# Moving the modulation's vector work between the stages of a two-layer transformer kernel

## The chip, the cores and the metric

The kernel runs on one core of a Trainium2 chip. The number that counts is the device time of one execution in microseconds. The work of one core is shared by five engines that run at the same time and wait for one another by semaphores: PE (TensorE, matrix products), DVE (VectorE, elementwise), ACT (ScalarE, elementwise and functions), POOL (GpSimd) and SP (SyncE, which here only issues the loads). [...]

## The reference, cut to what matters

The reference computes two layers over two streams of 256 tokens, the latent `lat` and the context `cx`, with 1024 channels. Every layer begins with modulation vectors, nine pieces of 1024 for each stream, which come from one large product; they give shift, scale and gate of the layer's three blocks.

```
for i in range(2):
    mod  = (silu(c)     @ mod_w[i] + mod_b[i]).reshape(bsz, 3, 3, 1, 1024)     # mod_w[i]: 1024 x 9216
    modc = (silu(c_ctx) @ mod_w[i] + mod_b[i]).reshape(3, 3, 1024)
    lat = lat + 0.5 * mod[:, 0, 2] * swiglu(modulate(lat, norm_g[i, 0], mod[:, 0, 0], mod[:, 0, 1]), w13[i, 0], w2[i, 0])
    ...                                               # the same for cx
    y   = short_conv_mixer(...)  if i == 0 else  gqa_mixer(...)
    lat = lat + mod[:, 1, 2] * y
    lat = lat + 0.5 * mod[:, 2, 2] * swiglu(modulate(lat, ...), w13[i, 1], w2[i, 1])

modulate(t, g, shift, scale) = rms(t, g) * (1 + scale) + shift
swiglu(h, w13, w2)           = (silu(gate) * up) @ w2,   gate, up = split(h @ w13)      # hidden 2816
```

Layer 0 has the convolution, layer 1 the attention (8 query heads of 128, 2 key heads, keys from both streams). The context is dropped after the attention of layer 1, so the last swiglu works on 256 tokens and every other on 512. All of it is in float32.

## The kernel before, in words

**Products.** Channels lie on the 128 partitions and tokens along the free axis. To keep float32 accuracy on PE, every operand is split into a high and a low half (`split`, L97 to L99: a copy on ACT makes the high half, a subtraction on DVE the low half), and one product is three matmuls (`mm3`, L122 to L124: high by high, high by low of the activations, low of the weights by high). A weight tile is loaded raw (`load_raw`, tiles `wr`, 1 MB each, three buffers, issued by SP), and its halves `wh` and `wl` (L98, L99) are the tiles that PE reads.

**Stages.** In order of time: a startup in which the first modulation pieces are computed on PE and the first norm is applied in four quarters (`norm_q`, which calls `norm_k`, L264 to L275), with PE's order written out by hand in `FIRST_STEPS`; swiglu (0, 0); the convolution, eight blocks of channels in one loop; its output projection; swiglu (0, 1); swiglu (1, 0); the attention with its projections; the projection by `wo`; and the last swiglu (1, 1).

**A swiglu** (`ffn`) has 22 blocks of 128 hidden channels, taken in thirds of 8, 7 and 7 (`THIRDS`). Each third makes its blocks of silu(gate) * up and then projects them back by `w2` (`project`). A block is made in one of two ways. Plain: 48 matmuls of 512 columns. As a block pair (class `Pair`): seven products of 256 columns, twelve matmuls each, in place of the eight half-products of a plain block; the operands are sums of weight blocks and sums of activation blocks. A pair's weight sums are made on DVE (`ws`, L564, L570, L574), then split like the others, so that PE does less for a pair and DVE more. The first third of swiglu (0, 0) has eight plain blocks: three that end the startup, and five of the loop `AS_IS`. The first third of (0, 1) and of (1, 0) has two plain blocks and six pairs, every later third has seven pairs. The last swiglu has plain blocks of 256 columns alone. So there are 14 pairs in (0, 0) and 20 each in (0, 1) and (1, 0), 54 in all.

**The modulation.** All pieces but the first two are computed on DVE, beside the rest. One operation (`mod_unit`, the tile `junk`, L142) multiplies a 128 x 1024 piece of the weights by silu(c) and adds along the row. There are 224 of them. A load of 1 MB (`modT`, through the same three `wr` buffers and the same SP queue as the other weights) feeds four of them, or two where only the latent stream needs the piece. Where they stand in the program is set by `tick(n)`: it adds n to what is owed, and issues as many whole operations as are owed. `mod_ready` issues whatever is missing before a piece is read. Ticks stand in the plain blocks' loop (L660), after the startup (L852), after each of the eight blocks of the convolution (L903), in `project` (argument `ev`, once for each of its first six or eight tiles), and in the attention (L1133, after each head, and a few others).

The order in the program is not the order on the engine. A scheduler places every engine's instructions by estimated readiness, and takes the program's order as priority; only PE's order in the startup is fixed by hand.

**The attention's heads** (L1127 to L1133). A head's scores go PE (`psc`), DVE (`mx`, `nb`), ACT (`e`, the exponential), DVE (`r`), POOL (`pn`, L1088, the only large use of POOL), PE (`pt`, a transpose), ACT and DVE (`pth`, `ptl`, the split), PE (`pav`). There are 16 such half heads. The weights of the projection that follows are split on DVE and ACT in the same time.

Of the kernel before, what the change touches and what calls it, by code (L numbers as in the profile page):

```python
# [20 lines left out]
T2 = 2 * S  # L21
# [20 lines left out]
def hybrid_kernel(ctx: ExitStack, tc: tile.TileContext, a: dict, out: bass.AP):  # L42
# [126 lines left out]
    def next_unit():  # L169
        if not units:  # L170
            l, ch, pair = jobs.pop(0)
            mod_tile(l, ch)
            raw = load_raw(a["modT"][l, ch * 4 + pair])
            units.extend(
                (l, ch, pair, raw, j, v) for j in range(2) for v in range(streams(l, ch))
            )
        mod_unit(*units.pop(0))

    def tick(n):

        owed[0] += n
        while (jobs or units) and owed[0] >= 1:
            owed[0] -= 1
            next_unit()
# [109 lines left out]
    def pick(h, k, c0, c1):  # L294
        return h.at(k, c0, c1)
# [92 lines left out]
    def new_pair(s):  # L388

        return (  # L390
            gp.tile([P, T2], F32R, name=nm(s + "h"), tag="gh"),
            gp.tile([P, T2], F32R, name=nm(s + "l"), tag="gl"),
        )
# [224 lines left out]
    def ffn(l, b, h, tot, gate, tail, gs=(), ev=1.5):  # L618
        gs = list(gs)
        i0 = 0  # L620
        for t, n in enumerate(THIRDS):
            between = ()
            if tot == T2:
                heads = []
                if t == 0 and not gs:

                    w = [load_w(a["w13"][l, b, 0])]
                    gs = [new_pair("g") for _ in range(2)]
                    pp = [(psum("pg"), psum("pu")) for _ in range(2)]
                    w13_mm(pp[0], w[0], h, range(KT), 0, S)  # L630
                    flush()
                    w.append(load_w(a["w13"][l, b, 1]))
                    w13_mm(pp[1], w[1], h, range(KT), 0, S)
                    h.sums(0)
                    w13_mm(pp[0], w[0], h, range(KT), S, T2)
                    w13_post(pp[0], gs[0], 0, T2)
                    heads.append(Pair(a["w13"][l, b, 2], h))
                    h.sums(1)
                    heads[0].sums(0)
                    w13_mm(pp[1], w[1], h, range(KT), S, T2)  # L640
                    w13_post(pp[1], gs[1], 0, T2)
                    heads[0].head()
                    h.sums(2)
                    heads[0].sums(1)
                prev = None
                for i in range(len(gs), n):
                    if t == 0 and not heads and i in AS_IS[l, b]:
                        w = load_w(a["w13"][l, b, i])
                        pp = psum("pg"), psum("pu")
                        if prev:  # L650
                            prev.seven()
                        w13_mm(pp, w, h, range(4), 0, T2)
                        if prev:
                            gs.append(new_pair("g"))
                            prev.four(gs[-1])
                            prev = None
                        w13_mm(pp, w, h, range(4, KT), 0, T2)
                        gs.append(new_pair("g"))
                        w13_post(pp, gs[-1], 0, T2)
                        tick(5)  # L660
                        continue
                    if heads:
                        pr = heads.pop(0)
                    else:
                        pr = Pair(a["w13"][l, b, i0 + i], h)
                        pr.sums(0)
                        pr.sums(1)
                        pr.head()
                    pr.five()
                    if prev:  # L670
                        prev.seven()
                    pr.six()
                    if prev:
                        gs.append(new_pair("g"))
                        prev.four(gs[-1])
                    prev = pr

                def last():
                    gs.append(new_pair("g"))
                    prev.four(gs[-1])  # L680

                between = (prev.seven, last) if prev else ()
            else:
                for i in range(n):
                    w = load_w(a["w13"][l, b, i0 + i])
                    gs.append(new_pair("g"))
                    pp = psum("pg"), psum("pu")
                    w13_mm(pp, w, h, range(KT), 0, tot)
                    w13_post(pp, gs[i], 0, tot)
                    tick(1)  # L690
            i0 += n
            box = {}

            def ws2(m):
                if m // 2 not in box:
                    src = a["w2a"][l, b, m // 2] if t == 0 else a["w2b"][l, b, t - 1, m // 2]
                    box[m // 2] = load_raw(src, 2 * n * P)
                raw = box[m // 2]
                o = (m % 2) * n * P
                hi, lo = half()  # L700
                split(hi[:, : n * P], lo[:, : n * P], raw[:, o : o + n * P])
                return lambda k: (hi[:, k * P : k * P + P], lo[:, k * P : k * P + P])

            cur = gs
            end = t == len(THIRDS) - 1
            project(
                ws2, lambda k, c0, c1: (cur[k][0][:, c0:c1], cur[k][1][:, c0:c1]), n,
                gate, tail if end else None, tot, 2 if end and tot == T2 else 0, ev, between,
            )
            gs = []  # L710

    def lazy_gate(l, j):
        box = []

        def get():
            if not box:
                box.append(gate_of(l, j))
            return box[0]

        return get  # L720


    h = Plain()
# [123 lines left out]
    h = FirstBlocks(h, h32)  # L847
# [1 line left out]
        gs0.append(new_pair("g"))  # L849
        w13_post(pps[i], gs0[i], 0, T2)  # L850
    h.sums()
    tick(6)  # L852

    convk = cload("convk", [P, 3, KT])
    qg = cload("qg", [P, 1])
# [5 lines left out]
    hn = Plain()  # L861
    ffn(0, 0, h, T2, lazy_gate(0, 0), tail_norm(0, 1, hn), gs0, 1.8)
    h = hn

    zs = []
    for m in range(KT):
        wcx = load_w(a["cw_cx"][m])
        if m % 2 == 0:
            wb = load_w(a["cw_b"][m // 2])
        pc, pv, pb = psum("pc"), psum("pv"), psum("pb")  # L870
        for c0, c1 in ((0, S), (S, T2)) if m == 0 else ((0, T2),):
            groups = ((pv, wcx, P), (pc, wcx, 0), (pb, wb, (m % 2) * P))
            if m == 0:
                order = [(k, *g) for k in range(KT) for g in groups]
            else:
                order = [(k, *g) for g in groups for k in range(KT)]
            for n, (k, ps, w, off) in enumerate(order):
                mm3(ps[:, c0:c1], w(k * 256 + off), pick(h, k, c0, c1), k == 0, k == KT - 1)
                if n == 11:
                    flush()  # L880
        xv = tp.tile([P, T2], F32, name=nm("xv"), tag="sg", bufs=3)
        nc.scalar.copy(xv, pv)
        u = tp.tile([P, T2], F32, name=nm("u"), tag="gm", bufs=3)
        nc.vector.tensor_tensor(out=u, in0=xv, in1=pc, op=ALU.mult)
        d = tp.tile([P, T2], F32, name=nm("d"), tag="gm", bufs=3)
        nc.vector.tensor_scalar(
            out=d, in0=u, scalar1=convk[:, 1, m : m + 1], scalar2=None, op0=ALU.mult
        )
        u2 = u.rearrange("p (s t) -> p s t", s=2)
        d2 = d.rearrange("p (s t) -> p s t", s=2)  # L890
        nc.vector.scalar_tensor_tensor(
            out=d2[:, :, 1:], in0=u2[:, :, : S - 1], scalar=convk[:, 0, m : m + 1],
            in1=d2[:, :, 1:], op0=ALU.mult, op1=ALU.add,
        )
        nc.vector.scalar_tensor_tensor(
            out=d2[:, :, : S - 1], in0=u2[:, :, 1:], scalar=convk[:, 2, m : m + 1],
            in1=d2[:, :, : S - 1], op0=ALU.mult, op1=ALU.add,
        )
        z = tp.tile([P, T2], F32, name=nm("z"), tag="sg", bufs=3)
        nc.vector.tensor_tensor(out=z, in0=d, in1=pb, op=ALU.mult)  # L900
        zs.append(new_pair("z"))
        split(zs[m][0], zs[m][1], z)
        tick(6)  # L903

    def by_pairs(key):
        box = {}
# [9 lines left out]
    hn = Blocks()  # L916
# [4 lines left out]
    h = hn  # L921
    hn = Blocks()
    ffn(0, 1, h, T2, lazy_gate(0, 2), tail_norm(1, 0, hn), (), 1.7)
    h = hn


    hn = Plain()
    ffn(1, 0, h, T2, lazy_gate(1, 0), tail_norm(1, 1, hn), (), 1.6)
    h = hn
    ap = ctx.enter_context(tc.tile_pool(name="ap", bufs=2))  # L930

# [195 lines left out]
    for hd in range(HEADS):  # L1127
        if hd + 2 < HEADS:
            pns[hd + 2] = scores(hd + 2)
        pts[hd] = turn(pns.pop(hd))  # L1130
        if hd:
            mix(hd - 1, pts.pop(hd - 1))
        tick(0.75)  # L1133
    mix(HEADS - 1, pts.pop(HEADS - 1))


    hn = Plain(S)
# [87 lines left out]
```

## Time and profile before

| what | value |
|---|---|
| time, median of 3 runs | 1597.02 us (1593.21 to 1598.21) |
| the profiled execution | 1595.53 us, its span 1593.7 us |
| PE busy | 1568.8 us, 98% of the span |
| DVE busy | 1303.3 us, 82% |
| ACT busy | 721.1 us, 45% |
| POOL busy | 29.4 us, 2% |
| modulation operations | 224, mean 1281 ns, 286.9 us of DVE |

A span is the time between the first and the last instruction of the profiled execution; the time of the run is 1.8 us longer. Busy shares are taken over the whole span. They say which engine has the most work, not where it stands still, and a stage can be bound by another engine than the whole: a stage's own busy times are read from a view by windows of time. In the views, "idle before" names what ended the idle time in front of a group of instructions.

### The profile page before, as it was taken

How to read it: one execution, taken by the hardware profiler on the slowest of the kernel's cores; microseconds unless marked ns; L12 is line 12 of the kernel's file. 1: busy time of each engine (PE TensorE's matmuls, PEld its weight loads, DVE VectorE, ACT ScalarE, POOL GpSimd, SP SyncE). 2: the span in 40 equal slices, each digit the busy share in tenths (PEclk: the TensorE clock that was granted, in tenths of full speed). 3: DMA queues.
4: the chain of work that ended last, by engine and by line, in shares of the span. 5: the costliest groups of instructions: out<-in, count | busy, mean ns of one | idle time of the engine just before them, and what ended most of it. 6: DMA issues, size and time to landing. Idle time of an engine off the chain costs nothing.

```text
span 1593.7 us, 25820 instructions
## 1 busy us (share of the span) xinstructions
PE 1568.8 (98%) x10666; PEld 1449.7 (91%) x10666; DVE 1303.3 (82%) x1984; ACT 721.1 (45%) x1103; POOL 29.4 (2%) x20
## 2 busy tenths in 40 slices
PE   8999999999999999999999999999999998899999
PEld 7688998999888899989899899899899897899999
DVE  5998888979999879798798879898797789876554
ACT  6522452544322356335345365335255455644443
POOL 0000000000000000000000000000000005200000
PEclk9999999999999999999999999999999999999999
DMA  9465324334565522452342513443433554556452
GB/s 359 181 238 207 110 99 153 133 102 176 177 219 195 175 68 93 148 170 100 129 156 96 180 56 107 158 136 99 169 118 120 208 186 151 200 185 220 166 200 102
DMA packets 39575, 248.79 MB, mean 156 GB/s; under 512 B 5409, under 2 KB 7201, under 8 KB 14625
## 3 DMA queue, kind: packets, MB, share of 16 engines
q1 hardware_dynamic: 36864, 245.38, 43.9%
q10 hardware_dynamic: 2592, 1.76, 0.4%
q8 instruction: 83, 1.36, 0.3%
q14 instruction: 36, 0.29, 0.1%
HBM read 244.77 MB, written 1.05 MB: 154 GB/s over the span
## 4 chain that ended last, share of the span: by engine, by line
PE 92%; DVE 4%; ACT 2%; DMA 1%; issue 0%; POOL 0%; ACTq 0%; DVEq 0%; POOLq 0%
PE py L123 10%; PE py L122 10%; PE py L124 10%; PE p L124 7%; PE p L123 7%; PE p L122 6%; PE q L122 5%; PE q L124 5%; PE q L123 5%; PE pg L122 2%; PE pg L124 2%; PE pg L123 2%; PE pu L124 2%; PE pu L123 2%; PE pu L122 2%; PE pv L122 1%
## 5 line engine op out<-in xcount | busy, mean ns | idle before, releaser
L98 ACT ACTIVATE wh<-wr 128x1024 fp32r<-128x1024 f32 (+2 forms) x276 | 276.4, 1014 | 388.0 <-PE py L123 140.7
L99 DVE TENSOR_TENSOR wl<-wr,wh 128x1024 fp32r<-128x1024 f32 (+2 forms) x276 | 319.9, 1166 | 88.2 <-ACT wh L98 87.9
L142 DVE CUSTOM_DVE_ANT_0 junk<-wr,scbc,modb 128x1024 bf16<-128x1024 f32 x224 | 286.9, 1281 | 31.8 <-DMA wr<-in_modT 29.0
L122 PE MATMUL py<-gh,wh 128*128 128x512 f32 (+1 forms) x746 | 263.3, 353 | 0.0
L123 PE MATMUL py<-gl,wh 128*128 128x512 f32 (+1 forms) x746 | 263.0, 353 | 0.0
L124 PE MATMUL py<-gh,wl 128*128 128x512 f32 (+1 forms) x746 | 262.7, 352 | 0.0
L99 DVE TENSOR_TENSOR wl<-ws,wh 128x1024 fp32r<-128x1024 f32 x108 | 131.6, 1223 | 34.1 <-ACT wh L98 34.0
L124 PEld LDWEIGHTS py<-gh,wl 128*128 128x128 f32 x746 | 141.1, 189 | 19.0
L122 PEld LDWEIGHTS py<-gh,wh 128*128 128x128 f32 x746 | 141.2, 189 | 18.6
L123 PEld LDWEIGHTS py<-gl,wh 128*128 128x128 f32 x746 | 141.2, 189 | 18.1
L98 ACT ACTIVATE wh<-ws 128x1024 fp32r<-128x1024 f32 x108 | 113.9, 1058 | 71.3 <-PE p L123 44.5
L124 PE MATMUL p<-th,wl 128*128 128x256 f32 x432 | 122.3, 283 | 0.0
L123 PE MATMUL p<-tl,wh 128*128 128x256 f32 x432 | 122.2, 283 | 0.0
L122 PE MATMUL p<-th,wh 128*128 128x256 f32 x432 | 122.2, 283 | 0.0
L453 DVE SCALAR_TENSOR_TENSOR x<-py,G,x 128x256 f32<-128x256 f32 x168 | 73.9, 477 | 23.1 <-PE py L124 23.1
L122 PE MATMUL q<-bh,wh 128*128 128x256 f32 x320 | 90.6, 283 | 0.0
L123 PE MATMUL q<-bl,wh 128*128 128x256 f32 x320 | 90.6, 283 | 0.0
L124 PE MATMUL q<-bh,wl 128*128 128x256 f32 x320 | 90.6, 283 | 0.0
L122 PEld LDWEIGHTS p<-th,wh 128*128 128x128 f32 x432 | 82.9, 192 | 0.3
L123 PEld LDWEIGHTS p<-tl,wh 128*128 128x128 f32 x432 | 82.9, 192 | 0.3
L124 PEld LDWEIGHTS p<-th,wl 128*128 128x128 f32 x432 | 82.9, 192 | 0.0
L124 PE MATMUL pg<-hh,wl 128*128 128x256 f32 (+1 forms) x240 | 75.5, 315 | 2.8 <-DVE wl L99 2.7
(236 smaller groups left out, 4045.2 us busy)
## 6 DMA issues: line engine op xcount, KB each, us to landing
wr<-in_w SPq DMA_DIRECT2D x88, 1024.0 KB, 4.9
wr<-in_modT SPq DMA_DIRECT2D x64, 1024.0 KB, 5.0
wr<-in_w2b SPq DMA_DIRECT2D x32, 896.0 KB, 4.6
wr<-in_w2a SPq DMA_DIRECT2D x16, 1024.0 KB, 4.9
pm<-in_mod SPq DMA_DIRECT2D x16, 512.0 KB, 10.0
wr<-in_cw_cx SPq DMA_DIRECT2D x8, 1024.0 KB, 4.9
wr<-in_cw_b SPq DMA_DIRECT2D x4, 1024.0 KB, 5.0
wr<-in_cw_out SPq DMA_DIRECT2D x4, 1024.0 KB, 4.9
```

What stands on the lines that cost most here:

```text
L98: nc.scalar.activation(out=hi, in_=src, func=AF.Copy)
L99: nc.vector.tensor_tensor(out=lo, in0=src, in1=hi.bitcast(F32), op=ALU.subtract)
L122: nc.tensor.matmul(ps, wh, mh, start=first, stop=False, **kw)
L123: nc.tensor.matmul(ps, wh, ml, start=False, stop=False, **kw)
L124: nc.tensor.matmul(ps, wl, mh, start=False, stop=last, **kw)
L142: nc.vector.tensor_tensor_reduce(out=junk, in0=raw[:, j * D : j * D + D], in1=scbc[:, v, :], scale=1.0, scalar=modb[:, l, col : col + 1], ...
L453: nc.vector.scalar_tensor_tensor(out=x[:, m, s * S : s * S + S], in0=ps[:, o : o + S], scalar=g[:, m, s : s + 1], in1=x[:, m, s * S : s * ...
```

## The change

Five places differ. In the plain blocks of the swiglus four operations of the modulation are issued after a block where there were five; this loop runs five times, in swiglu (0, 0). After each of the 54 block pairs a new half operation is owed, so one is issued after every second pair, 27 in all. After the startup four are issued where there were six; after each block of the convolution five where there were six; in the projections of swiglu (1, 0) 1.4 for each tile where there were 1.6 (22 tiles). After each attention head 0.75 was owed, six in all, and now none. Counted in the program's order these are 5 + 2 + 8 + 4.4 + 6 = 25.4 operations taken away and 27 added; the number of operations, of loads and of all other instructions on every engine is the same, since the last pieces are simply reached earlier or later.

```diff
@@ -657,7 +657,7 @@   (ffn, the plain blocks)
                         gs.append(new_pair("g"))
                         w13_post(pp, gs[-1], 0, T2)
-                        tick(5)
+                        tick(4)
                         continue
@@ -674,6 +674,7 @@   (ffn, the block pairs)
                         gs.append(new_pair("g"))
                         prev.four(gs[-1])
                     prev = pr
+                    tick(0.5)
@@ -849,7 +850,7 @@   (after the startup)
     h.sums()
-    tick(6)
+    tick(4)
@@ -900,7 +901,7 @@   (the convolution's loop)
         split(zs[m][0], zs[m][1], z)
-        tick(6)
+        tick(5)
@@ -925,7 +926,7 @@
-    ffn(1, 0, h, T2, lazy_gate(1, 0), tail_norm(1, 1, hn), (), 1.6)
+    ffn(1, 0, h, T2, lazy_gate(1, 0), tail_norm(1, 1, hn), (), 1.4)
@@ -1130,7 +1131,6 @@   (the attention's heads)
             mix(hd - 1, pts.pop(hd - 1))
-        tick(0.75)
```

## Prediction

> **What bounds the kernel now.** I read the page first, for the engines' work, the chain that ended last, and the operation that is moved.
>
> ```profile
> PE 1568.8 (98%) x10666; PEld 1449.7 (91%) x10666; DVE 1303.3 (82%) x1984; ACT 721.1 (45%) x1103; POOL 29.4 (2%) x20
> ...
> PE 92%; DVE 4%; ACT 2%; DMA 1%; issue 0%; POOL 0%; ACTq 0%; DVEq 0%; POOLq 0%
> ...
> L142 DVE CUSTOM_DVE_ANT_0 junk<-wr,scbc,modb 128x1024 bf16<-128x1024 f32 x224 | 286.9, 1281 | 31.8 <-DMA wr<-in_modT 29.0
> ```
>
> PE is the bound. Moving DVE work can only win back time in which PE stands, or make it stand. Taking the starts of all matmuls, and what each takes beyond its undisturbed 120 ns (256 columns) or 226 ns (512), I count 38.9 us of standing in all: some 20 in the startup, 9.3 in the attention's heads, 4 before the last swiglu, the rest in the passages between swiglus. So then the windows by stage: startup, seven pairs of (0, 0), six pairs of (0, 1), the heads.
>
> ```profile
> 0.00:78.00 78.00, 70.56 (x432) 53.98 (x433) 55.91 (x121) 45.65 (x88) 0.19 (x4) 0.96 0.73 275
> 172.50:240.30 67.80, 67.80 (x566) 67.79 (x565) 53.61 (x67) 38.05 (x59) 0.00 (x0) 1.00 0.29 96
> 598.20:656.00 57.80, 57.80 (x481) 57.67 (x481) 51.97 (x62) 34.52 (x55) 0.00 (x0) 1.00 0.29 101
> 1334.00:1367.00 33.00, 26.08 (x169) 20.91 (x167) 30.36 (x74) 23.82 (x53) 27.74 (x16) 1.00 0.42 150
> ```
>
> Columns are length, then PE, PEld, DVE, ACT and POOL busy, granted clock, DMA share, GB/s. Beside the pairs PE is full and DVE has 14.2 us free in 67.8, but only 5.8 in 57.8 at (0, 1). In the heads PE is busy 26.1 of 33.0 and DVE 30.4: there DVE and POOL hold PE. Last, timelines of the two places with most standing. Startup, DVE and then PE:
>
> ```profile
> 51.24 0.68 DVE L383 TENSOR_TENSOR hr<-hr,hr 128x512 f32<-128x512 f32 x1
> 51.85 1.28 DVE L142 CUSTOM_DVE_ANT_0 junk<-wr,scbc,modb 128x1024 bf16<-128x1024 f32 x1
> ...
> 57.04 0.16 DVE L774 TENSOR_TENSOR A<-pr,sb 128x4 f32<-128x4 f32 x1
> ...
> 57.31 1.28 DVE L142 CUSTOM_DVE_ANT_0 junk<-wr,scbc,modb 128x1024 bf16<-128x1024 f32 x1
> ...
> 71.93 1.22 DVE L99 TENSOR_TENSOR wl<-wr,wh 128x1024 fp32r<-128x1024 f32 x1
> ```
> ```profile
> 73.20 0.50 PE L124 MATMUL pg<-hh,wl 128*128 128x512 f32 x1 [2.70 <-DVE wl L99]
> ...
> 76.08 0.63 PE L123 MATMUL pu<-hl,wh 128*128 128x512 f32 x1
> ```
>
> Four operations of the modulation run in a row ahead of the last quarter's norm (L774), a fifth behind it; at the far end of that chain PE waits 2.7 us for a weight's low half, and then runs at half pace: starts 427 ns apart until 77.4, at a granted clock of 0.57. Heads, DVE and then POOL:
>
> ```profile
> 1350.53 1.28 DVE L142 CUSTOM_DVE_ANT_0 junk<-wr,scbc,modb 128x1024 bf16<-128x1024 f32 x1
> 1351.73 0.09 DVE L142 DVE_READ_ACCUMULATOR2_ANT mod<- 128x1 f32 x1
> 1351.74 0.16 DVE L1084 RECIPROCAL r<-sm 128x1 f32<-128x1 f32 x1
> 1351.82 0.20 DVE L1074 TENSOR_SCALAR nb<-mx,scq 128x1 f32<-128x1 f32 x1
> 1351.93 1.27 DVE L142 CUSTOM_DVE_ANT_0 junk<-wr,scbc,modb 128x1024 bf16<-128x1024 f32 x1
> ```
> ```profile
> 1352.07 4.11 POOL L1088 TENSOR_SCALAR pn<-e,r 128x512 f32<-128x512 f32 x2 [0.85 <-DVE nb L1074]
> ```
>
> One operation stands in front of `r`, which POOL needs, another in front of `ptl`, which PE needs.
>
> **The change part by part.** Order on the engines is that of the changed program as it builds. All counts of instructions stay; PE's order differs in some 260 of its matmuls, POOL's not at all; SP's 249 loads are the same with the modulation's moved among the weights'.
>
> *Startup (6 to 4).* Now eight operations run ahead of the last quarter's end (46.4 to 58.5); changed, four stand ahead of its L774, one ahead of its last `hl`, and one behind the `tl` chain. The two `wl` that PE waits for move ahead of a `gl` and a `gm`. The second `wl` (end 73.15) comes earlier by two operations (2.6), one `gl` and one `gm` (0.6 each): about 69.3. PE, 0.9 us earlier since the last quarter's norm ends sooner, would need it at 68.9. So of 0.9 (waits at 60.6 to 62.9) + 3.65 (69.8 to 73.5) + 2.0 (slow clock, 9 starts by 0.2) = 6.5 all but 0.4 goes. I take -6; ends -6.5 (all) and -2.6 (only the two operations). What is late next is that `wl`, by 0.4.
>
> [...]
>
> *Plain blocks (5 to 4), convolution (6 to 5).* PE has 51.0 of 51.6 us in the plain blocks, DVE 47.5. Five operations fewer win nothing where nothing waits: 0, ends -0.5 and 0. In the convolution 8 x 1.28 = 10 us leave DVE's 127.7 of 133; the weights there come 0.35 to 0.40 us before PE reads them, and no stretch of PE's starts is late. 0, ends -1 and 0.
>
> *Half an operation beside each pair.* 27 x 1.28 = 34.6 us of DVE. With 14.2 us free for seven pairs, three or four operations (4.5) fit. The built order has them in clusters near the beginning of each third's pairs. What counts is how early each weight half is written before PE's first read. In the stages of seven pairs that is 4.5 to 5 us nearly everywhere (one place 2.6), more than a cluster that leads a third, itself covered by the projection. 0 there. In (0, 1)'s first third it is 0.47, 0.21, 1.84 and 1.10 us at 605.0, 609.9, 611.0 and 617.5, while the pairs catch up; four operations now come into these pairs (5.1 against 5.8 free). Each costs up to 1.28 less its slack; 0.8, 1.1 and 0.2 make 2.1, and PE's changed order (the previous pair's seventh product between the current one's) gives up to 1.4 of cover. I take +0.5, nearer to the covered end; ends -1 and +3.8 (three uncovered). At the entry to (1, 0) four operations in the projection's tail push the first pair's sums into the norm (slacks there 0.10 to 0.62): +0.7, ends 0 and +2.5. (1.6 to 1.4 takes 4.4 operations out of stages with such slack: 0.)
>
> *Heads.* 33 us hold six operations, 7.7 us of DVE; one stays, and four splits of the next projection's weights, of which two ran here already, come up. DVE goes from 30.4 by -5 x 1.28 + 2 x 1.14 = -4.1 to 26.3, level with PE's 26.1. The other bound is POOL: 16 `pn` from 1332.5 to 1366.3, 33.8 us, 29.5 busy. One takes 1.56 us, but 2.5 to 2.7 in the four cases where it begins while a `junk` or a `wl` of 1.2 us is running (1.9 in a fifth). 16 x 1.56 + 2 x 1.0 = 27 and some 2.5 idle make 29.5, 4.3 less. I take -4; ends 0 (the waits only change their names) and -7.7 (all DVE time removed).
>
> [...]
>
> *Before the last swiglu.* At 1393.55 two `wl` (2.35 us) run ahead of the `ri` (L246) that the norm waits for; changed, one does. 1.14 us on the path, half taken since ACT and PE join the chain there: -0.6; ends -1.1 and 0.
>
> Sum: -6 + 0.5 + 0.7 - 4 - 0.6 = -9.4 on the profiled execution's 1595.5 (span 1593.7 and 1.8 around it): 1586.1. That execution is 1.5 below the median 1597.0; midway for the median, 1587.
>
> **The rivals.**
>
> *Heads give nothing.* POOL's chain of `r`, `pn`, `pt` sets the period, since scores of head n+2 wait for earlier buffers. For it: PE's longest waits there are for `pn` (3.0 us in three). Against it: `r` itself stands behind the operations. 1587 + 4 = 1591.
>
> *Startup gives nothing*, because the last quarter's data come late rather than the operations holding them. Against it: DVE idles 0.6 us in that stretch. 1593; with the heads' failure too, 1597.
>
> *Slower: loads beside the pairs.* Seven more modulation loads (27 / 4) take one of the three `wr` buffers beside pairs, which hold one each until their last block is split. If the next pair's weights wait for that buffer, four operations (5.1) and a landing (5.0 by the profile's median) come against 4.5 to 5 us of slack: about 5 us a load. Two of seven eat the gain, three make it measurably slower; half of them give 1587 + 17 = 1604. For it: the load is at the mercy of SP's order. Against it: DMA share there is 0.29.
>
> *The change does not do what it says.* The scheduler moves the operations, and here it does cluster them; were they all put where they stood, 1597.
>
> **How the numbers follow.** What can be told from no change is about 0.3%, 4.8 us. Forecast, 1584 to 1590: 0.46. Heads alone fail, 1591: 0.16. Startup alone fails, 1593: 0.08. Both, or the last rival, 1597: 0.12. Loads, from 1599 up: 0.13. All parts at their good ends, below 1584: 0.05. Faster: 0.46 + 0.16 + 0.05 and a third of 0.08 give 0.70; slower half of the loads' case and some accident, 0.13; the rest, 0.17. The range that leaves out 2 in 10 goes from 1581 to 1599.
>
> **What would show it.** Startup: no PE wait for `wl` above 1 us near 70 and a clock of 1.00 after it; the first pair's stage begins some 6 us earlier. Heads: from the first `pn` to the last about 30 us, no `junk` but one. Pairs: PE busy again for the whole of 57.8 and 67.8 us. Wrong would be: PE waits for `wl` or `ws` halves in the thirds, DVE idle for `modT` loads there, or `pn` still 33 us from first to last.

## The result

The changed kernel takes 1586.87 us (median of 5 runs, 1586.30 to 1589.18) against 1597.02 us before: a ratio of 0.9945, 95% interval 0.9934 to 0.9957. The forecast was 1587. A second set of runs on another occasion gave 0.9932 (0.9917 to 0.9946). The profiled execution took 1586.5 us, its span 1584.7.

The page of the changed kernel, engines, chain and the moved operation:

```profile
PE 1565.9 (99%) x10666; PEld 1448.4 (91%) x10666; DVE 1302.0 (82%) x1984; ACT 720.4 (45%) x1103; POOL 26.1 (2%) x20
...
PE 94%; DVE 2%; ACT 2%; DMA 1%; issue 0%; ACTq 0%; DVEq 0%
...
L142 DVE CUSTOM_DVE_ANT_0 junk<-wr,scbc,modb 128x1024 bf16<-128x1024 f32 x224 | 286.7, 1280 | 32.8 <-DMA wr<-in_modT 30.2
```

DVE's work is the same to 1.3 us; what shrank is its share of the chain, from 4% to 2%. PE's standing, counted as before from the starts of all matmuls, fell from 38.9 to 29.8 us. That is 9.0 of the 9.0 by which the spans differ, so the whole gain is PE's standing, as it had to be.

The total came out, but not the parts. This table is made from the starts of the matmuls, from one profiled execution each; "entry" is a swiglu's two plain blocks ahead of its pairs, "queries" the attention's projections up to the first `psc`, "heads" goes from there to the last `pav`, "`wo` and norm" from that `pav` to the first product of the last swiglu. All in us.

| stretch | before | changed | changed, 2nd profile | predicted change |
|---|---|---|---|---|
| to the first pair of (0, 0) | 172.42 | 165.48 | 164.91 | -6 |
| pairs and projections of (0, 0), convolution | 398.07 | 398.06 | 398.07 | 0 |
| entry to (0, 1) | 27.54 | 26.25 | 28.27 | 0 |
| the rest of (0, 1) | 323.53 | 323.86 | 323.85 | +0.5 |
| entry to (1, 0) | 29.15 | 27.37 | 27.54 | +0.7 |
| the rest of (1, 0) | 323.62 | 323.62 | 323.61 | 0 |
| queries and heads | 95.58 | 95.14 | 93.61 | -4 |
| `wo` and norm | 28.46 | 28.49 | 29.00 | -0.6 |
| last swiglu | 191.85 | 192.92 | 192.10 | 0 |

**Startup.** The timeline of the changed kernel, DVE and then PE (a line of the source behind the pairs' loop has a number one higher than before):

```profile
51.01 1.27 DVE L142 CUSTOM_DVE_ANT_0 junk<-wr,scbc,modb 128x1024 bf16<-128x1024 f32 x1
...
52.22 0.15 DVE L775 TENSOR_TENSOR A<-pr,sb 128x4 f32<-128x4 f32 x1
...
64.88 0.68 DVE L537 TENSOR_TENSOR gm<-sg,pu 128x512 f32<-128x512 f32 x1
65.48 2.35 DVE L99 TENSOR_TENSOR wl<-wr,wh 128x1024 fp32r<-128x1024 f32 x2
67.75 0.68 DVE L99 TENSOR_TENSOR gl<-gm,gh 128x512 fp32r<-128x512 f32 x1
```
```profile
67.58 0.39 PE L123 MATMUL pg<-hl,wh 128*128 128x512 f32 x1
67.89 0.50 PE L124 MATMUL pg<-hh,wl 128*128 128x512 f32 x1
```

The last quarter's norm begins at 52.2 and not at 57.0, both `wl` run in one piece and end at 67.8, and the product that waited 2.70 us starts without a wait. No stretch at half pace follows: the starts stay 0.23 us apart. The window of the first 78 us, with the same columns as before, shows PE busy 74.1 where it was 70.6, and a granted clock of 0.98 where it was 0.96:

```profile
0.00:78.00 78.00, 74.11 (x463) 57.70 (x464) 57.35 (x122) 45.69 (x88) 0.19 (x4) 0.98 0.73 279
1322.30:1355.80 33.50, 28.20 (x168) 22.87 (x167) 27.35 (x68) 22.24 (x50) 25.94 (x16) 0.95 0.32 112
```

**Heads.** The second line is the stretch of POOL's `pn`, first to last. It is 33.5 us long and was 33.8, although DVE has 27.4 us of work in it where it had some 31, and POOL 26. Its clock is 0.95: PE lost about 1.4 us at half pace in it. DVE and PE in the early heads:

```profile
1329.80 1.20 DVE L99 TENSOR_TENSOR wl<-wr,wh 128x1024 fp32r<-128x1024 f32 x1
1330.92 1.28 DVE L99 TENSOR_TENSOR ptl<-pt,pth 128x512 fp32r<-128x512 f32 x2
...
1332.30 1.21 DVE L99 TENSOR_TENSOR wl<-wr,wh 128x1024 fp32r<-128x1024 f32 x1
```
```profile
1330.22 0.38 PE L122 MATMUL pav<-pth,vh 128*128 128x256 f32 x1 [0.69 <-ACT e L1081]
1331.74 0.47 PE L122 MATMUL psc<-kh,qh 128*128 128x512 f32 x1 [1.14 <-DVE ptl L99]
```

The four `wl` of the next projection stand where operations of the modulation stood: at 5.2, 7.5 and 10.0 us into the stretch, and the first just ahead of it. PE waits 1.14 us for the `ptl` behind one of them. In the second profile of the same kernel the order is the same, the clock did not fall in the heads, and the stretch was 32.0.

**Pairs.** Seven pairs of (0, 0) with their last blocks, and six of (0, 1), in the changed kernel:

```profile
274.00:351.00 77.00, 77.00 (x616) 75.75 (x615) 67.70 (x90) 39.71 (x61) 0.00 (x0) 1.00 0.35 118
590.00:659.00 69.00, 69.00 (x541) 67.19 (x540) 63.90 (x82) 36.62 (x57) 0.00 (x0) 1.00 0.35 120
```

PE is busy in every part of both; DVE has come to 63.9 of 69.0 in the second. In this kernel the six pairs of (0, 1) take 0.3 us longer than before, and no other stretch of pairs does.

### The profile page after: what moved, and what is told of

Read it like the earlier page. It is cut to its first block, busy times and chain, and to the rows that moved or that the text cites. A ratio compares the mean times of both kernels' runs of the same rounds, so it can differ in the third digit from the quotient of the medians.

```text
span 1584.7 us, 25774 instructions
## 1 busy us (share of the span) xinstructions
PE 1565.9 (99%) x10666; PEld 1448.4 (91%) x10666; DVE 1302.0 (82%) x1984; ACT 720.4 (45%) x1103; POOL 26.1 (2%) x20
## 4 chain that ended last, share of the span: by engine, by line
PE 94%; DVE 2%; ACT 2%; DMA 1%; issue 0%; ACTq 0%; DVEq 0%
PE py L123 10%; PE py L124 10%; PE py L122 10%; PE p L124 7%; PE p L123 7%; PE p L122 7%; PE q L122 5%; PE q L124 5%; PE q L123 5%; PE pg L122 3%; PE pg L124 3%; PE pg L123 3%; PE pu L122 3%; PE pu L123 3%; PE pu L124 3%; PE pv L122 1%
## 5 line engine op out<-in xcount | busy, mean ns | idle before, releaser
L98 ACT ACTIVATE wh<-ws 128x1024 fp32r<-128x1024 f32 x108 | 113.7, 1058 | 79.6 <-PE p L123 33.8
L122 PE MATMUL pg<-hh,wh 128*128 128x256 f32 (+1 forms) x240 | 76.0, 317 | 2.7 <-ACT wh L98 1.6
```

Source lines behind the costliest of these rows:

```text
L98: nc.scalar.activation(out=hi, in_=src, func=AF.Copy)
L122: nc.tensor.matmul(ps, wh, mh, start=first, stop=False, **kw)
```

## The experiments

Twelve kernels ran in three sets, one of them the changed kernel once more. Each set has its own runs of the kernel before, to which the ratios refer.

### Single edits, and loads held back

The startup's edit alone:

```diff
     h.sums()
-    tick(6)
+    tick(4)
```

> The kernel before with one edit: four operations after the startup in place of six. Theory A (the prediction's sum): the second wl that PE waits for at 73.2 us lands near 69, the clock stays at 1.00, and the whole is 6 us faster than before, 1591 against 1597. Theory B (the gain of the changed kernel is the sum of several places, the startup one of them, as the two traces have it: 6.9 us): 6 to 7 faster. Rival C (the startup alone gives little, because the spans there differ from run to run by their first loads, 0.8 us and more): under 3 faster.

Measured: 1590.98 us, ratio 0.9973 (0.9963 to 0.9983), so 4.3 us faster (2.7 to 5.9). A's 6 and B's 6 to 7 lie above the interval, C's "under 3" reaches just into it. Its timeline names the difference to the changed kernel:

```profile
66.17 1.22 DVE L99 TENSOR_TENSOR wl<-wr,wh 128x1024 fp32r<-128x1024 f32 x1
67.30 0.68 DVE L537 TENSOR_TENSOR gm<-sg,pu 128x512 f32<-128x512 f32 x1
67.90 0.68 DVE L99 TENSOR_TENSOR gl<-gm,gh 128x512 fp32r<-128x512 f32 x1
68.50 1.22 DVE L99 TENSOR_TENSOR wl<-wr,wh 128x1024 fp32r<-128x1024 f32 x1
```
```profile
69.77 0.50 PE L124 MATMUL pg<-hh,wl 128*128 128x512 f32 x1 [1.11 <-DVE wl L99]
```

Here a `gm` and a `gl` still run between the two `wl`, and PE waits 1.11 us. The first loads of the program did not come at the same time in each execution (PE waited 3.0 us for `pm` before, and 0.8 and 1.3 us in the two profiles of the changed kernel), so the stage is best compared behind them, from the 73rd product `pg` or `pu` to the 161st (51.7 to 78.1 us before). That takes 26.1 to 26.4 us in the three kernels with neither edit (before, the pairs' edit alone, the heads' edit alone), 21.5 in this kernel and in the two-edit kernel below, and 20.0 to 20.3 in all nine profiles that also have four operations in the plain blocks. So the two edits together are worth 6.1 us: the startup's 4.8, and the plain blocks', which the prediction put at nothing, 1.2. The plain loop was changed together with others only, so this share rests on the stage's length and not on a run of that edit alone.

The heads' edit alone:

```diff
             mix(hd - 1, pts.pop(hd - 1))
-        tick(0.75)
```

> The kernel before without the operations after the attention's heads, all else as before. Theory A (the prediction's sum): the heads' stretch from the first to the last pn shrinks from 33.8 to about 29.5 us and the whole is 4 us faster. Theory B (read from the trace after, where that stretch is 33.5): the four weight splits of the next projection move into the first heads in place of the operations, the stretch stays within 1 us of 33.8, the whole is 0 to 1 us faster.

Measured: 1594.69, ratio 0.9995 (0.9984 to 1.0005): nothing. POOL's stretch is 32.9 us. The timeline of DVE in its heads shows why:

```profile
1351.09 1.29 DVE L142 CUSTOM_DVE_ANT_0 junk<-wr,scbc,modb 128x1024 bf16<-128x1024 f32 x1 [0.64 <-DMA wr<-in_modT]
...
1355.35 1.27 DVE L142 CUSTOM_DVE_ANT_0 junk<-wr,scbc,modb 128x1024 bf16<-128x1024 f32 x1
```

No tick asks for these two. In the program's order the last tick of the attention issues the 210th operation, and `mod_ready` then issues six at once behind the heads, for the scale of the last norm, since those that were taken away still have to be done; the scheduler lifts some of them back into the heads. From the first `psc` to the last `pav` there are 6 operations where there were 9, and behind it 11 where there were 8.

The pairs' edit alone:

```diff
                     prev = pr
+                    tick(0.5)
```

> The kernel before with half an operation after every block pair added, nothing taken away elsewhere. Theory A (the prediction's sum): +0.5 and +0.7 at the two entries, nothing in the other thirds: 1 us slower, so within the noise of before. The prediction's rival of the loads beside the pairs: about 17 us slower. Theory B: the pairs lose nothing, PE busy in the windows of six and seven pairs stays at their whole length, within 1.5 us of before either way, the rest set by whether the clock drops in the passages.

Measured: 1589.66, ratio 0.9967 (0.9955 to 0.9979): 5.3 us faster (3.3 to 7.2), where A expected a loss of 1 and B at most 1.5 either way. The pairs lose nothing (323.5 and 323.7 us for the two stretches that took 323.5 and 323.6), though the beginning of the convolution takes 1.0 us more. Most of what it gives lies far behind the edit: all 224 operations are done before the attention begins, though the ticks in the heads are still in the program, since nothing is left for them to issue. Queries and heads take 91.95 us where they took 95.58; 2.4 us of that lie ahead of the first `pn`, and 1.6 between the first `pn` and the last, which take 32.2 us where they took 33.8. Another 1.6 us lie at the entry to (1, 0), where the order of PE's products has changed; the startup's edit alone brings that too.

The loads of the first two weights by `wo` held back (shortened to the place in the heads' loop; the projection then takes the held tiles):

```diff
+        if hd in HOLD:                       # (1, 3)
+            raw = wp.tile([P, 2048], F32, name=nm("wr"), tag="wr", bufs=3)
+            nc.vector.tensor_copy(out=raw[:, :1], in_=aos[hd - 1][1][:, :1].bitcast(F32))
+            nc.sync.dma_start(raw, a["wo"][HOLD.index(hd)])
+            held[HOLD.index(hd)] = raw
```

> The changed kernel, with the first two loads of the weights by wo held back by one element that is written into each tile from a head's result (after the first and the third head), so that their four splits run in the middle and the late heads and not in the first ones. Theory A (no gain in the heads because POOL's chain sets their period anyway): within 0.7 us of the changed kernel, 1587. Theory B (the early splits cost about what the missing operations gave): the heads shrink by 2 to 3 us from 33.5 and the whole comes to 1584 to 1585.

Measured: 1584.15, ratio 0.9933 (0.9919 to 0.9946). That is the second measurement of the changed kernel itself, 0.9932. The splits did move (two to 18.9 and 23.3 us into the stretch, two behind its end) and the stretch is 32.0 us; but the changed kernel's second profile has 32.0 too, without any of this. The time is the one that B names, but the kernel before is 2 us faster in this set as well. The first profile's stretch was 1.5 us longer, with about 1.4 us lost at half pace in it. Nothing here supports B.

### Which edits carry the gain

The changed kernel itself, for a ratio in this set:

> The changed kernel itself, unaltered, beside the others of this set on the same chip. Every theory: its ratio to the kernel before again near 0.9945, that is 8 to 10 us faster.

Measured: 1586.26, ratio 0.9932 (0.9917 to 0.9946), as expected.

Two edits alone, the startup's `tick(4)` and the pairs' `tick(0.5)`, all else as before:

> Two edits alone: four operations after the startup, and half an operation after every pair; plain blocks, convolution, the 1.4 and the heads as before. Theory B (the startup's edit gives 4 to 6, the pairs' edit 5, since the 27 operations done there are missing later, in the attention and behind it, and the remaining edits give nothing): 9 to 10 us faster than before, like the whole change, and no operation in the heads. Theory A (each edit gives at its own place, the heads' part comes from the heads' edit): 5 to 6 faster.

Measured: 1586.80, ratio 0.9938 (0.9924 to 0.9953): the whole gain, to within the 2 us or so that the intervals leave. B holds in the sum. In the parts the two kernels differ: this one begins its pairs 2.6 us later than the changed kernel beside it (167.5 against 164.9; 1.2 of it behind the first loads), loses 0.7 us more in the convolution and 1.5 in (0, 1) and (1, 0) behind their entries, and has queries and heads shorter (91.9 against 93.6), since it has no operation left there at all.

The changed kernel without the pairs' edit:

```diff
                     prev = pr
-                    tick(0.5)
```

> The changed kernel without the half operations beside the pairs. Theory B (the operations taken away come back where the pieces are needed, in the late heads, in the projection by wo and in its norm, where PE has no other work): the stretch from the last pav to the last swiglu's first product gets longer than the changed kernel's 28.5 us by 2 us or more, the whole is 5 to 10 us slower than the changed kernel. Theory A (the pairs' part costs 1 us and the rest gains): 1 us faster than the changed kernel.

Measured: 1591.14, ratio 0.9966 (0.9953 to 0.9979), so 5.4 us slower than the changed kernel by the ratios. From the last `pav` to the first product of the last swiglu it takes 31.5 us, 3.0 more than the 28.5 (2.5 more than the 29.0 of the changed kernel's profile in this set). The rest of (1, 0) takes 1.9 us more. In the program's order `mod_ready` issues 11 operations in one piece at the gate of (1, 0) and 14 at the last norm, where the changed kernel forces none. The longest wait of PE and the timeline of DVE at that norm:

```profile
PE pg L122 <- ACT hh L274: 5.0, 1, 5.0
```
```profile
1387.45 1.28 DVE L142 CUSTOM_DVE_ANT_0 junk<-wr,scbc,modb 128x1024 bf16<-128x1024 f32 x1
...
1388.78 1.28 DVE L142 CUSTOM_DVE_ANT_0 junk<-wr,scbc,modb 128x1024 bf16<-128x1024 f32 x1
...
1391.12 0.16 DVE L197 SCALAR_TENSOR_TENSOR A<-mod,normg 128x8 f32<-128x8 f32 x1
...
1392.34 1.25 DVE L264 SCALAR_TENSOR_TENSOR t<-x,A,ss 128x256 f32<-128x256 f32 x3
```

The last norm's scale (L197) stands behind operations that it needs, the norm behind the scale, and the first product waits 5.0 us for it. Operations taken away early come back where they are needed, and there PE has nothing else to do.

How many operations run where (counted in the profiles; a stretch of pairs is taken from 2 us before its first product to its last):

| kernel | pairs | queries | heads | behind the heads |
|---|---|---|---|---|
| before | 37 | 7 | 9 | 8 |
| changed | 53 | 7 | 3 | 6 |
| heads' edit alone | 37 | 7 | 6 | 11 |
| pairs' edit alone | 53 | 0 | 0 | 0 |
| changed, without the pairs' edit | 35 | 7 | 6 | 19 |

### The clock behind the last norm

In every profile but one, products run for a while at half pace behind some of the passages in which PE stands. The changed kernel behind the last norm:

```profile
1388.27 0.58 PE L122 MATMUL pg<-hh,wh 128*128 128x256 f32 x1 [1.11 <-ACT hh L274]
1388.65 0.42 PE L122 MATMUL pu<-hh,wh 128*128 128x256 f32 x1
1388.87 0.41 PE L122 MATMUL pg<-hh,wh 128*128 128x256 f32 x1
```

Starts are 0.21 us apart and not 0.12, until 1394.0, at a granted clock of 0.50 (1388 to 1394 us), which loses 2.4 us. So idle matmuls were put into that norm, 8 and 12 of 128 columns, writing an unused part of the tile that holds the sums (shortened; a second loop stands behind the inverse):

```diff
+        for _ in range(8):
+            nc.tensor.matmul(pq[:, :P], ident, ident, start=True, stop=True)
         rs = tp.tile([P, 2], F32, name=nm("rs"), tag="rs")
```

> The changed kernel with 20 idle matmuls of 128 columns (0.11 us each) into an unused part of a PSUM tile in the norm ahead of the last swiglu, 8 between the sums and their inverse and 12 between the inverse and the first product, where PE stands 0.9 and 1.6 us. Theory C (PE's idle share in these 5 us lowers the granted clock, and the 2.4 us that PE loses behind it from 1388.7 to 1394.0 is that clock's cost): the clock behind the norm stays at 1.00 and the whole is 1 to 2 us faster than the changed kernel. Rival (the clock falls whatever PE does there, or the added matmuls only stand in the way): no faster, or up to 0.5 us slower.

Measured: 1590.57, ratio 0.9961 (0.9949 to 0.9973), some 4.6 us slower than the changed kernel by the ratios. The products behind the norm run at full pace, but the clock had fallen ahead of them: it is at 0.50 from 1388.4 to 1395.2 us, while the idle matmuls run. Besides, the inverse's `rs` reads the same tile and waited for the idle matmuls: DVE's `ri` stood 3.00 us for it. That is a flaw of the experiment. The second form writes a tile of its own, 4 behind the sums and 7 behind the inverse:

> The changed kernel with idle matmuls (0.22 us each) in a PSUM tile of their own, so that nothing reads or waits for it: 4 behind the sums of the last norm, 7 behind its inverse. Theory C (PE's idle share in the 5 us of that norm lowers the clock behind it, 1.6 to 2.4 us lost at half pace in the changed kernel's profiles): no stretch of starts 0.21 us apart behind the norm, 1 to 2 us faster than the changed kernel, ratio to before near 0.993. Rival: the idle matmuls cost their own time and the clock falls at another moment, no faster.

Measured: 1586.07, ratio 0.9936 (0.9919 to 0.9954): no faster. PE in that norm:

```profile
1387.23 1.14 PE L244 MATMUL spare<-ident,sq 128*128 128x128 f32 x8
...
1388.92 3.09 PE L263 MATMUL spare<-ident,ri 128*128 128x128 f32 x14
1391.76 0.36 PE L122 MATMUL pg<-hh,wh 128*128 128x256 f32 x1
```

Each idle matmul counts as two instructions here; the second group takes 0.22 us for each, against 0.12 to 0.14 in the first group, so it ran at about half pace already. The half pace was spent on the idle matmuls instead: the first 30 products then take 3.7 us and not 5.5 to 6.3, but the passage takes 7.6 us and not 5.6 to 6.1. The sum is even. By these profiles theory C is right in what the clock costs, but it isn't bought back in this way.

Both at once, held loads and idle matmuls:

> The same idle matmuls, and the loads of the first weights by wo held back until the first and third head. Theory B with C: 2 to 4 us faster than the changed kernel, 1583 against 1587, ratio near 0.991. Rival (the held loads gave nothing: the changed kernel's heads took 32.0 us too in the profile in which the clock did not fall in them, like the 32.0 with held loads): as with the idle matmuls alone.

Measured: 1585.57 (1581.76 to 1589.00), ratio 0.9936 (0.9917 to 0.9955), no different from the changed kernel. Its profiled execution, at 1581.76 (span 1580.0, granted clock 0.999), was the only one of fourteen in which no product behind the startup ran at half pace. Even there the clock fell once, to 0.51 from 1382.1 to 1385.5 us, under the idle matmuls.

No version here beats the changed kernel beyond what its runs can tell.

### How much fits beside the pairs

One and two operations behind each pair, in place of a half:

```diff
-                    tick(0.5)
+                    tick(1)
```

(and `tick(2)` in the second.)

> The changed kernel with one operation after each pair in place of a half. Theory B (DVE's free time beside the pairs is the limit): 7 operations take 9.0 of the 14.2 us free in a third of seven pairs, no loss there; 6 take 7.7 of 5.8 us in the first third of (0, 1), a loss of 2 us or so. With the attention already free of operations there is nothing more to win: 1 to 3 us slower than the changed kernel. Rival (the earlier the better): 1 us or more faster.

Measured: 1588.99, ratio 0.9957 (0.9941 to 0.9972). Against the changed kernel's ratios of 0.9945 and 0.9932 in other sets that is 2 to 4 us slower, with intervals that overlap, so B's 1 to 3 is not contradicted. In the profile the convolution's beginning is 1.0 us longer, the rest of (0, 1) 0.4 and the rest of (1, 0) 2.0. The loss of 2 us that B put into the first third of (0, 1) came in the first third of (1, 0).

> The changed kernel with two operations after each pair. Theory B: 14 operations of 1.28 us are 17.9 us against 14.2 free in a third of seven pairs and 15.4 against 5.8 in the first third of (0, 1): PE waits some 4 us in each third of (0, 0) and later ones until the operations run out, 10 or so in the first of (0, 1), in all 15 to 25 us slower than the changed kernel. Rival (the scheduler carries the surplus into the projections, where DVE has more free time): under 5 us slower.

Measured: 1594.47, ratio 0.9995 (0.9984 to 1.0006): all of the gain is lost, 8 to 10 us by the ratios. Pairs and projections of (0, 0) take 5.3 us more, the rest of (0, 1) 7.1, the rest of (1, 0) 2.5. The window of the third third of (0, 0), which takes 81 us where it took 77:

```profile
274.00:355.00 81.00, 79.07 (x616) 76.36 (x615) 78.09 (x107) 40.92 (x63) 0.00 (x0) 1.00 0.45 153
```
```profile
318.96 0.39 PE L124 MATMUL q<-th,wl 128*128 128x256 f32 x1 [0.52 <-DVE wl L99]
```

DVE is busy 78.1 of 81 us and PE waits for `wl`. Beside these stretches of pairs there are 13, 16, 11, 16 and 15 operations and not 14 or 12 in each, so the scheduler levels them. The cost does not follow that count alone: against the changed kernel those five stretches lose 0, 3.7, 1.9, 0.2 and 3.5 us. The expected 15 to 25 us were too many: the first third of (0, 1) did not lose 10.

## Why the prediction was right, and where it was not

**The sum held, to 0.1 us in the median; of the two largest steps one held and one did not. That the total fits so closely is luck.** The gain is 8.8 us (6.9 to 10.5) by the first set's ratio. PE's standing was the place to look, and it was the whole of it.

*Startup, -6.* Right in place, chain and size: 57.0 to 52.2 for the last quarter, `wl` done at 67.8 (69.3 was worked out), PE's need at 67.9, no wait, no fall of the clock; the stage is 6.9 to 7.5 us shorter, 6.1 of it behind the first loads, whose waits differ between executions by a microsecond either way (0.8 to 3.0 us for `pm`). Wrong was which edit does it. The step gave all to 6 to 4 and nothing to the plain blocks' 5 to 4, since nothing waits in those blocks; but that edit also changes the order on DVE ahead of them, where PE waits. Alone, 6 to 4 gives 4.8 there and leaves 1.11 of the wait.

*Heads, -4.* The step failed. It counted five operations out of the heads as if taken out, and counted two of the coming four splits as new; the heads were measured as a stage between 0.4 shorter (first profile, queries included) and 2.0 (second). The edit to which it was put gives nothing by itself, for the operations come back as forced ones. What the step also left out is that the splits of `wo` come in the first heads, where operations stood, and are not spread over them. Its sum for POOL had POOL's work nearly right, 27 us where 26.2 were measured, but let its idle time between the first `pn` and the last shrink from 4.3 us to 2.5 without a reason; it grew to 7.3 and 5.8. In the changed kernel one `pn` takes 2.5 us, the one that begins under a `wl`, against four of 2.5 to 2.7 before. So POOL was freed of 3.3 us and the stretch gained at most 1.8. Even with no operation in the heads, in the pairs' edit alone, it takes 32.2 us; what sets these 32 us is not shown.

*Before the last swiglu, -0.6.* Failed: 28.46 us became 28.49 and 29.00. One `wl` did leave the norm, but two operations now stand ahead of the last `acc`, for which PE waits 1.24 us, in place of the 1.22 that it waited there for ACT's `sq`.

*Pairs, +0.5 and +0.7, and nothing in the sevens.* The costs were right in kind: 0.3 us in (0, 1) and 0 in (1, 0) and (0, 0). They are not fixed to the edit: the pairs' edit alone costs nothing in (0, 1), the two-edit kernel 0.5 there and 1.0 in (1, 0). The entry to (1, 0) got shorter by 1.8 where +0.7 was expected. There the step overlooked PE's order. Before, the norm's product `ss` (L252) comes behind 41 products of the plain blocks, DVE stands for it, and PE then waits 1.06 us for a `bl` that DVE writes behind that norm:

```profile
934.42 2.83 DVE L264 SCALAR_TENSOR_TENSOR t<-x,A,ss 128x256 f32<-128x256 f32 x7 [5.22 <-PE ss L252]
```

In the changed kernel `ss` comes ahead of those products, and the wait for `bl` is gone, as it is with the startup's or the pairs' edit alone, but not with the heads'. What was wrong is the view of the step: it took the pairs for a cost alone, with the gain at the places from which operations go. By the runs the pairs carry much of it: 5.3 us alone, and 5.4 lost when they are taken out of the change. Every operation done there is one fewer at the end of the list, and the end of the list lies in the attention and behind it.

*The rivals.* That the heads give nothing, at 1591, was about right for the heads and wrong for the time. The loads beside the pairs cost nothing at this number. That the change does not do what it says has a grain: the heads' edit does not.

So the sum came out of a startup worth 6.1 us and 0.8 to 1.4 more by the chance of the first loads, two steps of together -4.6 that gave 0.4 to 1.4, an entry to (1, 0) that gave 1.6 to 1.8 where a loss was set down, and two passages that differ between the profiles of the changed kernel (the entry to (0, 1), 26.25 and 28.27 us, and the last swiglu, 192.92 and 192.10) and that gave 0.2 in one and cost 1.0 in the other. Errors of both signs cancelled. By the experiments on single edits the same sum reads otherwise: 4.3 from the startup's edit and 5.3 from the pairs', each with the new order at the entry to (1, 0) in it.

## What to carry to other kernels

Where work is handed out from one list beside other work, an edit at one place moves everything that is later in the list: ask where the list ends, and what the last items delay. Work taken away early is not gone; here the pieces that a late norm needed were issued in front of it and held PE for 5.0 us. Put such work beside the stage in which the engine that bounds is never waiting and the other has time free, up to that time and no further: half an operation for each pair fits here, two take back the gain.

## What the runs showed of the hardware

- The clock fell in short passages, and not in the same ones each time. In the profiles of before and of the changed kernel nine falls to 0.50 began and ended within the program, seven of 3.41 us and two of 6.83. From 1384 to 1389 us of the changed kernel PE was busy 2.65 of 5.00 us at a granted clock of 0.84, and from 1388 to 1394 us the clock was 0.50. From 568 to 582 us it was 0.88 before and with the pairs' edit alone, and 1.00 in the changed kernel and with the startup's edit alone. Counting stretches of starts at half pace after the first 60 us, the profiles lose some 0 to 7 us (about 5 before and in both profiles of the changed kernel, 7 with the heads' edit alone, none in the fastest). One stretch costs 0.8 to 2.5 us. The entry to (0, 1) of the changed kernel took 26.25 us in one profile, with waits of 0.66, 0.26 and 0.84 us and full pace, and 28.27 in the other, with 1.17, 0.26 and 0.84 and 1.4 us lost at half pace. What decides whether a passage brings a fall was not shown.
- A `pn` on POOL takes 1.56 us in most cases. It took 2.5 to 2.7 (1.0 to 1.1 us more) in the five that began under a `junk` or `wl` of 1024 columns of which 1.1 to 1.3 us were left, four before and one in the changed kernel, and 1.56 where such an instruction began in its course: the one at 1337.92 in the profile of before overlaps a `junk` for 0.85 us and takes 1.56. The `wl` at 1327.46 of the changed kernel, which begins 0.2 us behind a `pn`, takes 1.56 us where others take 1.21. What lengthens them was not shown.
- The idle matmuls in a tile of their own moved the half pace to themselves: with 22 instructions in the last norm, 1.8 to 2.6 us were won behind the norm and 1.5 to 2.0 lost in it.
